# A decoder block on one core: the head's transfers in a fixed order, the mixing stage with `u` projected first, five gate tiles in one piece

## The chip, the core and the metric

The kernel runs on one core of a Trainium2 chip. The core's engines work side by side, each through an instruction list of its own: TensorE (PE, matrix products into PSUM), VectorE (DVE), ScalarE (ACT), GpSimd (POOL) and SyncE (SP, which here only issues transfers). Sixteen DMA engines move data between DRAM and SBUF. An instruction waits until the semaphores of what it needs have come; whatever stands behind it on the same engine waits with it.

The metric is the device time of one launch in microseconds (us), as the median of several runs. Besides, one execution is taken with the hardware profiler; all durations of single instructions come from that execution.

## The reference

One layer of a decoder over 512 tokens of width 1024, in fp32:

```
h = h + 1/2 * SwiGLU_1(RMSNorm(h))                 # ffn1, inner width 2816
z = RMSNorm(h) @ W_in                              # q | six k/v | branch gates | u
o = concat(NSA(q, k/v, gates), S5(u))              # 8 heads x 64  |  32 groups x 16 channels
h = h + o @ W_out
h = h + 1/2 * SwiGLU_2(RMSNorm(h))                 # ffn2
h = h + sigmoid(RMSNorm(h) @ W_gate) * (p @ W_ple)
out = RMSNorm(h)
```

NSA is an attention with three branches (compressed, selected and window keys), whose outputs are mixed by sigmoid gates. Its compressed keys come from a small network over windows of 32 tokens ("compression"). S5 is a complex linear recurrence over time with 64 states for each group of 16 channels, followed by a gelu and a gated product `y * sigmoid(y @ w_glu + b_glu)`.

## The kernel before

**Data.** `h` stays in SBUF for the whole run, transposed: 8 parts (`KT`) of 128 channels by 512 tokens. All weights lie in one DRAM array, `wpack`, in the order of use, cut into *units* of 128 x 1024 fp32 (512 KB). `load_unit` (L104) transfers one into a ring of four raw buffers; `unit` and `split` (L135 to L153) then make two matrices of it, `hi` (ScalarE, L151, the value rounded to the format that TensorE reads) and `lo = raw - hi` (VectorE, L152). The activations are split in the same way: `xh` on ScalarE, `xl` on VectorE (`split_k`, L171). Each product then is three products (`mm3`): hi by xh, hi by xl, lo by xh. One tile of 128 outputs by 512 tokens from 1024 inputs is 24 products of 512 columns, and closes a PSUM bank (tags A to D). Every product of the kernel is issued by the helper `mm`, so that all have line 130.

**Norms.** The split takes `h` times the gain; the scale of each token is put on later, after the product, where linearity allows it. `square` (L176) sums the squares of the parts on an adder (GpSimd in the head, VectorE elsewhere), `finish` (L190) sums over partitions by four small products on TensorE, takes the root (`rsqrt_steps`, L309) and spreads the result `rb` over all partitions by one more.

**Stages**, with their place in the profiled execution: the head (first transfers, splits and products, 0 to about 50 us), ffn1 (to 382; the constants of S5 are computed on VectorE beside it), the mixing stage (from the first `w_in` products, about 373, to about 621), the output projection and `p @ W_ple` (to about 655), ffn2 (to 998), the gate (998 to 1049) and the last norm and output (to 1063).

**The head.** Program order is unit 0, the eight parts of `h`, units 1 to 3 (L114 to L121). Unit 0 alone is split in two halves, so that products with its first half need not wait for all of it. The squares of parts 0 to 7 are added by seven steps on GpSimd (L184). VectorE also begins the chain of S5 constants here: small steps of 128 x 32 (L525 to L536, L552 and so on) on `prm`. The S5 tensor `s5o` in DRAM gets zeros by seven transfers that SP issues (L649).

**The mixing stage** (`mixer`, L794 to L1343) is written as Python generators, each step of which issues some instructions, and which `weave`, `chain` and `drain` interleave:
- `kq` (L969): two tiles of K with rotary embedding (six VectorE steps on 128 x 512 each, L959 to L964, a trip through DRAM, four `KA` copies and four `KB` subtractions, L976 and L977), then the first pair of Q tiles; `rotary(qd[1], "B")` is the second pair.
- `s5_input` (L852): four tiles of `u`; each is scaled (`ut`, L856), written to DRAM and read back as `u8` in another layout.
- `s5_in` and `s5_out` (L882, L910), for each of eight blocks of four groups: small products `ps_C<-u,fi`, eight VectorE steps on 256 columns (L894 to L897, L904 to L907), four scans (L900), then 16 small products and a copy; every second block `s5_back` (L923) transposes the output back.
- `cmp_kv` and `v_gates`: the remaining tiles of `w_in`. `cmp_all`: the compression. `glu` (L1079): first a gelu over S5's output and its split, then four tiles of the gated product, twelve products each.
- `scores` (L1121), for blocks 3 and 2 in one buffer pool and 1 and 0 later: products of Q with K in halves `QA,KA` (128 rows: 64 of hi and 64 of lo) and `QB,KB` (112 rows: 64 and 48 rows of an added term), a maximum on VectorE (L1155) and an exponential on ScalarE.
- `compressed`, `shifts`, `values`: the rest of the attention. `out_half`: the output projection, of which half the products (S5's half, `fill`) are put among the last steps of the attention.

In the kernel before the order is `kq`; the tiles of `u`; the second Q pair; then S5 woven with the scores of blocks 3 and 2, `cmp_kv` and `v_gates`; then the compression, with the gated product behind it.

**The gate** (L1396 to L1438): eight tiles of `sigmoid(norm(h) @ W_gate) * ple`, each in two halves of 256 tokens, all eight tiles for the first half and then all eight backwards for the second (which keeps eight split units in SBUF), so that the first half's last norm, scaling and output run beside the products of the second half.

**What sets the order.** `ENGINE_ORDER` lists, for each of the five engines, the positions of its instructions in the program as moves (step, and count of neighbours: `65:45` goes 65 ahead and takes 45 in a row), and `impose` (L1639) chains them:

```
            for _ in range(int(count or 1)):
                if before is not None:
                    tc.add_manual_dep(traced[at], before.name, follow, reason="order")
                before = traced[at]
                at += 1
```

So the generators above give the program's numbering and the buffers, while the list gives what an engine does first. `TILE_ORDER` adds pairs between engines. A transfer is an entry of SP's list like any other.

## Time and profile before

| | |
|---|---|
| median of 3 runs | 1063.21 us (1060.61 to 1064.24) |
| the profiled execution, its own time | 1064.68 us |
| its span | 1062.9 us |
| its granted TensorE clock | 0.986 |
| TensorE busy | 1026.4 us (97%), 6398 instructions |
| VectorE busy | 814.2 us (77%), 1369 instructions |
| ScalarE busy | 524.7 us (49%), 917 instructions |
| GpSimd busy | 81.9 us (8%), 100 instructions |
| DMA packets moved | 146.94 MB, mean 138 GB/s |

The span is the time from the first to the last recorded instruction; the execution's own time lies 1.8 us above it. The busy share is taken over the whole span and says little on one stage: the page therefore cuts the span into 40 slices of 26.6 us and gives a digit for each (9 is 90% or more), with the clock that TensorE was granted in tenths below. A window gives the same in us for any stretch. In the windows and groups "x" is a count; the mean of one instruction is given in ns; "idle before" is how long the engine did nothing ahead of it, with what ended the wait behind the arrow. The length of a TensorE instruction in the timeline is longer than its share of the pipeline: the distance between neighbouring starts is what counts.

### The profile page before, as it was taken

To read this page: it belongs to the slowest core of one execution; us is meant where nothing else is said; L and a number is where in the kernel's file an instruction comes from. 1 tells how busy PE (TensorE), PEld (TensorE's weight loads), DVE (VectorE), ACT (ScalarE), POOL (GpSimd) and SP (SyncE) were. 2 spreads that over 40 slices of the span, in tenths; PEclk is the share of its full clock that TensorE was granted. 3 is DMA by queue.
4 is the path that set the end of the run, shared out by engine and by line. 5 is a ranking of instruction groups with operands and counts; after the bars stand their busy time and mean duration, and the time that the engine had idled before them with its cause. 6 is when DMAs were issued, how large, how long until landed. Compare 5 with 4: busy or idle time off the path is not lost.

```text
span 1062.9 us, 16719 instructions
## 1 busy us (share of the span) xinstructions
PE 1026.4 (97%) x6398; PEld 899.3 (85%) x6398; DVE 814.2 (77%) x1369; ACT 524.7 (49%) x917; POOL 81.9 (8%) x100
## 2 busy tenths in 40 slices
PE   5999999999999999999899999999999999999995
PEld 4788899889989888886677787998899899899895
DVE  7799979777987675799798987875576467576776
ACT  5244256436425532257789856553355245245532
POOL 4000010001010100000000001001010001000000
PEclk9899999999999999999799999999999999999998
DMA  8332456757546836878210055447365545646202
GB/s 296 98 101 83 106 137 166 234 131 161 173 130 171 272 122 187 201 213 254 61 37 24 21 179 162 111 119 201 73 147 158 140 110 119 169 110 183 87 1 80
DMA packets 72128, 146.94 MB, mean 138 GB/s; under 512 B 19424, under 2 KB 30688, under 8 KB 71792
## 3 DMA queue, kind: packets, MB, share of 16 engines
q1 hardware_dynamic: 60512, 127.05, 38.4%
q0 software_dynamic: 10688, 18.65, 10.9%
q8 instruction: 50, 0.82, 0.3%
q10 hardware_dynamic: 848, 0.17, 0.1%
q14 instruction: 30, 0.25, 0.1%
HBM read 121.17 MB, written 15.73 MB: 129 GB/s over the span
## 4 chain that ended last, share of the span: by engine, by line
PE 86%; DVE 8%; issue 2%; ACT 2%; DMA 1%; POOL 0%; SPq 0%; POOLq 0%; DVEq 0%; ACTq 0%
PE ps_C L130 27%; PE ps_B L130 23%; PE ps_A L130 22%; PE ps_D L130 14%; DVE nmax L1155 1%; DVE lo L152 1%; DVE vv L900 1%; ACT xh L173 0%; DMA ti<-s5t 0%; DMA raw<-in_wpack 0%; DMA u<-ud 0%; PE ps_C L676 0%; ACT xn L183 0%; DMA h<-in_xT 0%; ACT hi L151 0%
## 5 line engine op out<-in xcount | busy, mean ns | idle before, releaser
L151 ACT CAST hi<-raw 128x1024 fp32r<-128x1024 f32 (+2 forms) x203 | 209.8, 1043 | 237.8 <-PE ps_C L130 92.7
L152 DVE TENSOR_TENSOR lo<-raw,hi 128x1024 fp32r<-128x1024 f32 (+2 forms) x203 | 243.3, 1210 | 44.4 <-ACT hi L151 43.4
L130 PE MATMUL ps_C<-hq,hi 128*128 128x512 f32 x704 | 218.6, 392 | 0.0
L130 PE MATMUL ps_A<-xh,hi 128*128 128x256 f32 (+1 forms) x456 | 142.6, 313 | 10.4 <-ACT hi L151 10.4
L130 PE MATMUL ps_A<-xh,lo 128*128 128x256 f32 (+1 forms) x456 | 142.5, 312 | 5.7 <-DVE lo L152 5.7
L130 PEld LDWEIGHTS ps_C<-hq,hi 128*128 128x128 f32 x704 | 127.1, 188 | 23.5 <-issue 0.8
L130 PE MATMUL ps_A<-xl,hi 128*128 128x256 f32 (+1 forms) x456 | 142.5, 312 | 0.0
L130 PE MATMUL ps_C<-hq,lo 128*128 128x512 f32 x352 | 137.2, 390 | 0.0
L130 PEld LDWEIGHTS ps_A<-xh,hi 128*128 128x128 f32 x456 | 87.2, 191 | 16.0 <-ACT hi L151 10.4
L130 PEld LDWEIGHTS ps_A<-xh,lo 128*128 128x128 f32 x456 | 87.4, 192 | 11.3 <-DVE lo L152 6.6
L130 PEld LDWEIGHTS ps_A<-xl,hi 128*128 128x128 f32 x456 | 87.2, 191 | 5.8 <-DVE xl L282 0.3
L130 PE MATMUL ps_B<-sh,hi 128*128 128x256 f32 x280 | 79.2, 283 | 0.0
L478 DVE SCALAR_TENSOR_TENSOR h<-ps_C,h 128x512 f32<-128x512 f32 x64 | 43.9, 688 | 45.9 <-PE ps_C L130 45.8
L130 PE MATMUL ps_B<-sl,hi 128*128 128x256 f32 x280 | 78.8, 281 | 0.0
L130 PE MATMUL ps_B<-sh,lo 128*128 128x256 f32 x280 | 78.4, 280 | 0.0
L130 PEld LDWEIGHTS ps_C<-hq,lo 128*128 128x128 f32 x352 | 66.1, 188 | 14.2
L354 POOL DMA_DIRECT2D raw<-in_wpack x35 | 31.6, 904 | 492.2 <-ACT sq L183 243.8
L130 PE MATMUL ps_D<-sh,hi 128*128 128x256 f32 x220 | 62.2, 283 | 0.0
L130 PE MATMUL ps_D<-sl,hi 128*128 128x256 f32 x220 | 61.9, 281 | 0.0
L130 PE MATMUL ps_D<-sh,lo 128*128 128x256 f32 x220 | 61.7, 280 | 0.0
L130 PE MATMUL ps_B<-xh,hi 128*128 128x512 f32 (+1 forms) x164 | 58.2, 356 | 0.0
L130 PE MATMUL ps_B<-xh,lo 128*128 128x512 f32 (+1 forms) x160 | 55.8, 349 | 0.0
(402 smaller groups left out, 2319.7 us busy)
## 6 DMA issues: line engine op xcount, KB each, us to landing
raw<-in_wpack SPq DMA_DIRECT2D x172, 512.0 KB, 4.2
raw<-in_wpack POOLq DMA_DIRECT2D x35, 256.0 KB, 4.7
raw<-raw POOLq DMA_DIRECT2D x35, 256.0 KB, 3.3
so<-s5o SPq DMA_DIRECT2D x8, 512.0 KB, 5.5
h<-in_xT SPq DMA_DIRECT2D x8, 256.0 KB, 4.9
s5f<-fs SPq DMA_DIRECT2D x4, 512.0 KB, 4.4
s5o<-gt SPq DMA_DIRECT2D x4, 512.0 KB, 3.5
s5t<-tcs SPq DMA_DIRECT2D x2, 1024.0 KB, 5.6
```

The source lines that it names most:

```text
L130: return PE.matmul(o, lhsT, rhs, start=start, stop=stop, **kw)
L151: S.copy(hi[:, c], raw[:, c])
L152: V.tensor_tensor(lo[:, c], raw[:, c], hi[:, c].bitcast(F32), OP.subtract)
L354: nc.gpsimd.dma_start(a0[:, 1], src[:, 0:512], accum_op=OP.add)
L478: V.scalar_tensor_tensor(h[:, m, :], o, 0.5, h[:, m, :], OP.mult, OP.add)
L900: V.tensor_tensor_scan(vv[:, g], r8[:, GC * j + g:GC * j + g + 1].to_broadcast([128, 64]), t1[:, g], 0.0, OP.mult, OP.add)
L1155: V.tensor_reduce(mc, s_, AX.X, OP.max, negate=True)
```

## The change

The program text changes in four places, and all lists of `ENGINE_ORDER` and `TILE_ORDER` are new.

**1. The head.** Ten small products of a matrix of ones with itself stand at the start of TensorE's list.

```diff
     for k in range(KT):
         nc.sync.dma_start(h[:, k, :], xv[:, k, :])
-        if k == 5:
-            load_unit(1, nc.sync)
+    load_unit(1, nc.sync)
     load_unit(2, nc.sync)
...
+    early = bank("D", (128, 128))
+    for _ in range(WARM):
+        mm(early, ones, ones, True, True)
...
+WARM = 10
```

In the lists: SP issued five parts of `h`, unit 0, a part, `prm`, unit 4 (which has a buffer outside the ring), two parts, unit 1, five zero writes, unit 2, small constants and zero writes, unit 3. After, it issues unit 0, part 0, unit 4, parts 1 to 7, units 1, 2 and 3, then `prm`, the other constants and units 5 to 8 of the list, and the seven zero writes behind these. ScalarE begins with one half of unit 0's `hi`, the square and `xh` of part 0 and the other half, and takes the squares of three parts among the first ten steps; part 7's `xh` is its fourteenth step. VectorE's splits of units 1 and 2 stand ahead of the chain of S5 constants (before: unit 2's behind its first half). GpSimd's seven additions stay as they are, behind squares that come earlier.

**2. The mixing stage.**

```diff
         def s5_input():
             for m in range(4):
                 o = proj("AD"[m % 2])
+                if m == 0:
+                    nm.finish()
+                    for t, raw in zip((cosr, sinr), ropes):
+                        V.tensor_tensor(t, raw, nm.rb, OP.mult)
...
-        drain(kq())
-        s5g, pg, cg, gg = s5_all(), chain(cmp_kv(), v_gates()), cmp_all(), glu()
-        sg = chain(scores(3, envs[3], mp, TS, G3), scores(2, envs[2], mp, "BC", G2))
+        s5g, pg, cg, gg = s5_all(), chain(kq(), rotary(qd[1], "B"), cmp_kv(), v_gates()), cmp_all(), glu()
+        s3, s2 = scores(3, envs[3], mp, TS, G3), scores(2, envs[2], mp, TS2, G2)
         drain(s5_input())
-        drain(rotary(qd[1], "B"))
         S.preload_act_table_set("exp_and_others")
-        weave((s5g, 17), (sg, S1), (pg, 6))
+        weave((s5g, 17), (pg, PROJ))
+        drain(pg)
         drain(s5g)
-        drain(pg)
-        drain(sg)
+        next(gg)
         s5x.close()
...
-        for _ in range(8):
-            next(cg)
+        next(s3)
+        next(s2)
+        sg = chain(s3, s2)
+        cg = chain(gg, cg)
+        weave((sg, S1), (cg, 12))
+        drain(sg)
```

The units of `wpack` stand in the new order of use. In TensorE's list: three products of `u` and the last 21 of ffn1's down projection; the rest of the 96 products of `u` with the five of the norm, and 42 of K and of the first Q pair; then S5's eight blocks beside the rest of K and Q, `cmp_kv` and `v_gates`. Behind S5's last block stand the first gated tile (12 products), nine products of the second, and only then the first scores, which alternate with the gated product and then the compression. More products of `fill` than before stand ahead of the attention's last blocks, and none is left between the last value products, where nine stood.

**3. Rows of the second K half.** `KB`, `KBc`, `QB` and `orow` are filled to 128 partitions (16 rows of zeros more), and all products with them read 128 rows instead of 112.

```diff
-                    mm(s_[:, i], QB[0:112, h0 + i], KBg[0:112, g, rs, :nk], False, False)
+                    mm(s_[:, i], QB[:, h0 + i], KBg[:, g, rs, :nk], False, False)
```

**4. The gate.** Five tiles are computed over all 512 tokens; the last three in two halves, as before.

```diff
+        whole = slice(0, SEQ)
+        for m in range(GATE_FULL):
+            if m:
+                gate_w.append(unit())
+            tile_of(m, whole, "AB"[m % 2], m == 0)
+            squared(m, whole, False)
+        for m in range(GATE_FULL, KT):
+            gate_w.append(unit(keep=gp))
         for hf in range(2):
             cs = slice(hf * HS, hf * HS + HS)
...
+            for m in range(GATE_FULL, KT):
+                tile_of(m, cs, "AB"[(m + hf) % 2], False)
+                sq = squared(m, cs, m == KT - 1)
             _, pb = rsqrt_rows([acc[:, cs], sq], 2)
...
+GATE_FULL = 5
```

`tile_of` and `squared` are the body of the old loop as functions of tile and columns. The gate thus issues 120 products of 512 columns and 144 of 256 where it issued 384 of 256 (120 fewer; ten come with the head). In the lists, the first gate tile's products are mixed with the last blocks of ffn2, and of the first half's eight final scaling steps five stand between the steps of the second half's last norm.

The lists of ffn1 and ffn2 are new as well, with the same instructions in them.

More of the change, by code (lines that the diff above doesn't have):

```diff
@@ L809, in mixer @@
         nc.scalar.dma_start(sel, a["sel"])
-        orow = mp.tile([48, 3], F32, name="orow")
+        orow = mp.tile([64, 3], F32, name="orow")
         nc.scalar.dma_start(orow, a["orow"])
@@ L820, in mixer @@
         for br in range(2):
-            V.tensor_copy(KB[64:112, 2 * br:2 * br + 2, :],
-                          orow[:, br + 1:br + 2, None].to_broadcast([48, 2, SEQ]))
+            V.tensor_copy(KB[64:128, 2 * br:2 * br + 2, :],
+                          orow[:, br + 1:br + 2, None].to_broadcast([64, 2, SEQ]))
         zero = mp.tile([128, 1], F32, name="zero")
@@ L951, in rotary @@
             oa = proj(tag)
-            if not hasattr(nm, "rb"):
-                nm.finish()
-                for t, raw in zip((cosr, sinr), ropes):
-                    V.tensor_tensor(t, raw, nm.rb, OP.mult)
             yield
@@ L1138, in scores @@
                                        OP.mult, OP.subtract)
-            S.copy(QB[64:112].rearrange("p h q -> p (h q)"), zero[64:112, 0:1].to_broadcast([48, 1024]))
+            S.copy(QB[64:128].rearrange("p h q -> p (h q)"), zero[64:128, 0:1].to_broadcast([64, 1024]))
             env.update(QA=QA, QB=QB)
@@ L1297, in mixer @@
         s1, s0 = scores(1, envs[1], ap_, "B"), scores(0, envs[0], ap_, "B")
-        for _ in range(8):
-            next(cg)
+        next(s3)
[4 more added lines that the diff above has]
+        drain(sg)
         next(s1)
         next(s0)
-        next(gg)
         drain(cg)
         c32 = compressed(3, 2)
-        for _ in range(2):
-            next(c32)
-            next(gg)
         cc = tp.tile([128, SEQ], FR, tag="rb1", name="cc")[:, :192].rearrange("p (q a c) -> p q a c", q=4, a=2)
@@ L1311, in mixer @@
         shifts(2, 4)
-        drain(gg)
         sg = chain(s1, compressed(1), s0, compressed(0))
@@ L1398, in block_kernel @@
         pad(gp, PADS[2])
-        gate_w = [unit(keep=gp)]
+        gate_w = [unit()]
         gf = gp.tile([128, KT], F32, tag="gf", name="gf", bufs=1)
@@ L1408, in block_kernel, with tile_of @@
         HS = SEQ // 2
+        def tile_of(m, cs, tag, first):
+            n = cs.stop - cs.start
+            wu = gate_w[m]
+            o = bank(tag)[:, :n]
+            for k in range(KT):
+                sl = slice(k * 128, (k + 1) * 128)
+                mm3(o, wu[0][:, sl], wu[1][:, sl], ng.xh[:, k, cs], ng.xl[:, k, cs], k == 0, k == KT - 1)
+            if first:
+                ng.finish()
+            t = gp.tile([128, SEQ], F32, tag="gt", name="gt")[:, :n]
+            V.tensor_tensor(t, o, ng.rb[:, cs], OP.mult)
+            S.activation(t, t, AF.Sigmoid)
+            V.tensor_tensor(t, t, ple[:, m, cs], OP.mult)
+            V.tensor_tensor(h[:, m, cs], h[:, m, cs], t, OP.add)
@@ new lines, in squared @@
+        def squared(m, cs, last):
+            n = cs.stop - cs.start
+            if m == 0:
+                S.activation(acc[:, cs], h[:, m, cs], AF.Square)
+                return None
+            sq = gp.tile([128, SEQ], F32, tag="gsq", name="gsq")[:, :n]
+            S.activation(sq, h[:, m, cs], AF.Square)
+            if not last:
+                V.tensor_tensor(acc[:, cs], acc[:, cs], sq, OP.add)
+            return sq
+        whole = slice(0, SEQ)
[4 more added lines that the diff above has]
+            squared(m, whole, False)
@@ L1409, in block_kernel @@
+        for m in range(GATE_FULL, KT):
+            gate_w.append(unit(keep=gp))
         for hf in range(2):
             cs = slice(hf * HS, hf * HS + HS)
-            for i in range(KT):
-                m = i if hf == 0 else KT - 1 - i
-                if hf == 0 and m:
-                    gate_w.append(unit(keep=gp if m < KT - 3 else None))
-                wu = gate_w[m]
-                o = bank("AB"[i % 2])[:, :HS]
-                for k in range(KT):
-                    sl = slice(k * 128, (k + 1) * 128)
-                    mm3(o, wu[0][:, sl], wu[1][:, sl], ng.xh[:, k, cs], ng.xl[:, k, cs], k == 0, k == KT - 1)
-                if i == 0 and hf == 0:
-                    ng.finish()
-                t = gp.tile([128, HS], F32, tag="gt", name="gt")
-                V.tensor_tensor(t, o, ng.rb[:, cs], OP.mult)
-                S.activation(t, t, AF.Sigmoid)
-                V.tensor_tensor(t, t, ple[:, m, cs], OP.mult)
-                V.tensor_tensor(h[:, m, cs], h[:, m, cs], t, OP.add)
-                if i == 0:
-                    S.activation(acc[:, cs], h[:, m, cs], AF.Square)
-                else:
-                    sq = gp.tile([128, HS], F32, tag="gsq", name="gsq")
-                    S.activation(sq, h[:, m, cs], AF.Square)
-                    if i < KT - 1:
-                        V.tensor_tensor(acc[:, cs], acc[:, cs], sq, OP.add)
@@ L1454 @@
 G2 = "r3", "ra"
-TW, TY, TP, TS = "C", "D", "D", "B"
-S1 = 34
+TW, TY, TP, TS, TS2 = "C", "D", "D", "B", "BC"
+PROJ = 12
+WARM = 10
+S1 = 32
 DEBUG_STOP = None
@@ L1695, in _pack_weights @@
     kk = np.concatenate([ks, kw], axis=1).reshape(D_MODEL, 4, 2, 32)
+    for m in range(4):
+        up_tile(u, m)
     for half in range(2):
@@ L1698, in _pack_weights @@
     for pair in range(2):
-        if pair:
-            for m in range(4):
-                up_tile(u, m)
         for half in range(2):
@@ L1709, in _pack_weights @@
     add(vt[:, 6:8])
+    m_major(x["s5_w_glu"][0], range(4), range(4))
     wk, wv = (x[n][0].reshape(16, 128, 256).transpose(1, 0, 2) for n in ("cmp_wk1", "cmp_wv1"))
@@ L1713, in _pack_weights @@
         add(np.concatenate([wk[:, 2 * i:2 * i + 2], wv[:, 2 * i:2 * i + 2]], axis=1))
-    m_major(x["s5_w_glu"][0], range(4), range(4))
     m_major(x["w_out"][0], range(8), range(4, 8))
@@ L1747, in prep @@
     sel = (rows[:, None] % 8 == np.arange(8)[None, :]).astype(f32)
-    orow = ((rows[:, None] // 8) % 3 == np.arange(3)[None, :]).astype(f32)
+    orow = np.concatenate([((rows[:, None] // 8) % 3 == np.arange(3)[None, :]).astype(f32), np.zeros((16, 3), f32)])
     def dup(v):
```

8 lines of the change are left out of this document (4 added, 4 removed), and 315 rows, old and new, of tables (ENGINE_ORDER, TILE_ORDER).

## The prediction

> **What bounds the kernel now.** I read the page first, then the windows of the stages that the change touches, then single rows. From the page: the busy tenths of TensorE (PE) and VectorE (DVE), the granted clock, and the chain of work that ended last.
>
> ```profile
> PE   5999999999999999999899999999999999999995
> DVE  7799979777987675799798987875576467576776
> PEclk9899999999999999999799999999999999999998
> PE 86%; DVE 8%; issue 2%; ACT 2%; DMA 1%; POOL 0%; SPq 0%; POOLq 0%; DVEq 0%; ACTq 0%
> ```
>
> The chain is 86% TensorE. The only slices below 9 are the first, the twentieth (505 to 531 us) and the last, and the clock falls to 7 or 8 tenths at the same places or next to them. So a change of order can win only what TensorE loses: the head, the mixing stage and the end. The windows give busy time and, in brackets, instructions for each engine, then the granted clock, the DMA share and GB/s.
>
> ```profile
> core 0: us, PE busy (x) PEld busy (x) DVE busy (x) ACT busy (x) POOL busy (x), PEclk, DMA share, GB/s
> 0.00:10.43 10.43, 0.00 (x0) 0.00 (x1) 3.92 (x10) 6.65 (x11) 1.70 (x9) 1.00 0.81 293
> 10.43:16.57 6.14, 6.14 (x15) 4.75 (x15) 5.90 (x19) 5.87 (x10) 0.19 (x1) 1.00 1.03 252
> 16.57:23.88 7.31, 7.31 (x34) 6.03 (x32) 7.10 (x10) 1.40 (x2) 6.92 (x6) 1.00 1.02 361
> 23.88:28.31 4.43, 0.39 (x2) 0.00 (x0) 4.36 (x9) 0.70 (x1) 2.45 (x2) 0.83 0.35 141
> 28.31:31.66 3.35, 3.35 (x8) 2.67 (x9) 3.04 (x15) 0.39 (x1) 0.00 (x0) 0.50 0.50 159
> 60.00:100.00 40.00, 40.00 (x179) 33.10 (x178) 37.50 (x98) 17.43 (x22) 0.00 (x0) 1.00 0.28 82
> 382.00:436.00 54.00, 54.00 (x241) 44.25 (x240) 34.56 (x53) 15.07 (x17) 1.75 (x2) 1.00 0.55 158
> 436.00:512.00 76.00, 69.93 (x511) 53.57 (x511) 73.54 (x170) 43.98 (x106) 0.00 (x0) 0.97 0.76 216
> 512.00:541.00 29.00, 26.60 (x151) 20.86 (x152) 22.30 (x55) 22.18 (x49) 0.00 (x0) 0.83 0.14 38
> 541.00:616.00 75.00, 75.00 (x367) 56.24 (x366) 68.38 (x133) 65.20 (x159) 0.00 (x0) 1.00 0.10 29
> 1000.00:1049.00 49.00, 48.28 (x402) 47.66 (x402) 37.50 (x89) 19.70 (x38) 1.73 (x2) 1.00 0.20 65
> ```
>
> Two things stand here. The head does no product for 10.43 us and then stalls again from 23.88 to 28.31. In the mixing stage VectorE has slack in one window and none in the next: 34.56 of 54 us before 436, then 73.54 of 76 us (0.968). Between 436 and 512 VectorE is the bound, with TensorE waiting for it. From 512 to 541 both wait on a chain of small steps (VectorE 0.77, clock 0.83).
>
> **The head.** Timeline rows: start, length, engine, line, what it writes and reads, and in brackets the idle time before it and its releaser.
>
> ```profile
> 7.71 5.93 SPq L649 DMA_DIRECT2D s5o<-zz  x5
> 13.68 0.63 SPq L111 DMA_DIRECT2D raw<-in_wpack  x1
> 3.77 1.28 ACT L173 ACT_TABLE_LOAD   x1 [3.77 <-DMA h<-in_xT]
> 5.06 1.97 ACT L173 ACTIVATE xh<-h,gains 128x512 fp32r<-128x512 f32 x3
> 10.43 0.79 PE L130 MATMUL ps_A<-xh,hi 128*128 128x512 f32 x1 [10.43 <-ACT hi L151]
> 27.04 1.22 DVE L152 TENSOR_TENSOR lo<-raw,hi 128x1024 fp32r<-128x1024 f32 x1
> 28.31 0.79 PE L130 MATMUL ps_A<-xh,lo 128*128 128x512 f32 x1 [4.04 <-DVE lo L152]
> 16.38 10.03 POOL L184 TENSOR_TENSOR acc<-acc,xn 128x512 f32<-128x512 f32 x7 [10.37 <-ACT xn L183]
> 18.26 1.34 DVE L536 SCALAR_TENSOR_TENSOR dt<-prm,ex 128x32 f32<-128x32 f32 x1
> 29.07 0.19 DVE L536 SCALAR_TENSOR_TENSOR r<-x,ex 128x32 f32<-128x32 f32 x1
> 100.60 23.80 PE ps_C L130 x105
> ```
>
> The last row, from the chain, prices a full product (512 columns): 23.80/105 = 0.227 us. TensorE loses before: 10.43 to the first product; 6.14 - 15 x 0.227 = 2.7 on 15 products at half clock; 4.43 - 2 x 0.227 = 4.0 in the stall; 3.35 - 8 x 0.227 = 1.5 at half clock behind it; less 0.4 in 16.57 to 23.88, where 34 products took 7.31 us. Sum 18.2.
>
> After: unit 0 is the first transfer. The first `h` part landed by 3.77 (it released the table load); a unit is twice its bytes, at 293 GB/s 0.9 us more, so 4.6. Table load to 5.9; ScalarE's list then has half of `hi`, a square, `xh` of part 0 and the other half. At 1.97/3 = 0.66 each that is 2.6: first product at 8.5. The part-7 `xh` is the 14th ScalarE step: 5.9 + 9.2 = 15.1, its `xl` 0.75 behind (estimate from the rows of the same size), so tile A closes at 15.9; its 24 products need 5.4, so 2.0 are lost on supply. Unit 1's `hi` follows at 16.1 and its `lo` at 17.3: 1.4 lost. The stall at 23.88 goes: units 2 and 3 were issued behind zero writes that held SP's queue for 5.93 us (the first row), now ahead of them, and unit 2's `lo` (27.04) now stands ahead of the S5 constants on VectorE. What is late next is the squares' sums on GpSimd, beside which a small VectorE step took 1.34 us (18.26) and alone 0.19 (29.07); the adds now start about 7 us earlier, on the splits. I charge one such wait, 1.2. Lost after: 8.5 + 2.0 + 1.4 + 1.2 = 13.1, **gain 5**. Bounds: 8 with no supply loss behind the first product, 1 if four adds lie on the path (4 x 1.15 more). The next use of what the moved zero writes write lies far behind the head; I cost them at nothing.
>
> The warm-up products cost nothing (TensorE is empty). Were the clock at half for the first 6 us, 15 products would be done at 14.6 and nine more by 16.7: they save 0.8, since supply sets the end of A.
> [...]
>
> **The mixing stage.** Down's last product; S5's first products (a tile's view: count, ns min/median/max, first and last start); its last ones (the chain); the gated product's first wait; then VectorE groups before 436 (three rows; count, busy, mean ns, idle before) and between 436 and 512 (three).
>
> ```profile
> 381.56 0.39 PE L130 MATMUL ps_C<-hq,lo 128*128 128x512 f32 x1
> L130 PE MATMUL ps_C<-u,fi x32: 217/275/276, 436.1 to 456.7; 128*128 128x64 f32 x32
> 511.98 1.91 PE ps_D L130 x16
> 509.10 0.79 PE L130 MATMUL ps_A<-ol,hi 128*128 128x512 f32 x1 [3.37 <-DVE ol L1085]
> L152 DVE TENSOR_TENSOR lo<-raw,hi 128x1024 fp32r<-128x1024 f32 x10 | 12.1, 1212 | 0.2 <-ACT hi L151 0.2
> L977 DVE TENSOR_TENSOR KB<-kf,KA 64x512 fp32r<-64x512 f32 x4 | 2.6, 678 | 0.2 <-ACT KA L976 0.2
> L963 DVE TENSOR_TENSOR r<-r,rb 128x512 f32<-128x512 f32 x2 | 1.4, 688 | 0.0
> L900 DVE TENSOR_TENSOR_SCAN vv<-r,t 128x64 f32<-128x64 f32 x32 | 7.4, 274 | 0.2
> L896 DVE TENSOR_TENSOR t<-ps_C,ti 64x256 f32<-64x256 f32 x8 | 3.4, 426 | 0.1
> L152 DVE TENSOR_TENSOR lo<-raw,hi 128x840 fp32r<-128x840 f32 (+2 forms) x5 | 5.2, 1048 | 0.1
> ```
>
> Down's last product starts at 381.56, with nine of the first projection's among it; after, three of `u`'s: down ends at 381.79 - 6 x 0.227 = 380.4. Then stand 93 products of `u`, 42 of K and Q and five of the norm ahead of S5's first: 135 x 0.227 + 1.4 = 32, so S5 starts at 412.4 instead of 436.1, into the window where VectorE idled 19.4 us. What moves behind that start is four splits (4.8), four `KB` copies (2.7) and eleven rotary steps at 0.688 (7.6; four more lay behind 436 already): 15.1 us. VectorE's work from there to 616 is then 73.54 + 22.30 + 68.38 + 15.1 = 179.3. Packed as 436 to 616 was before (164.2/180 = 0.912), the 110.9 ahead of the attention take 121.6 and the attention its 75: 412.4 + 196.6 = 609.0. Packed at 0.968, as between 436 and 512: 114.6 + 75, 602.0. Without idle, attention included: 591.7. What speaks for the better packing is that the gated product now lies beside the scores, so that the sparse stretch 512 to 541 gets company; against it, that TensorE has some 59 us of products beside S5 itself (sum of my own count of the list, at these prices), about as much as VectorE there. From 616 come off 7.0, 14.0 and 24.3. Output products that filled the end of the attention are pulled ahead, and nothing of the kind is left there: nine of them, 1.5 to 2 us, are charged. **Gain 8**, between the first two; bounds 0 (the rival below) and 22.
>
> The rows of the second K half go from 112 to 128 partitions: no instruction and no column more. No row differs in that alone; I take nothing, bounds 2 us either way (a tenth of 0.227 on some hundred products). The two ffn lists are rewritten without other work: nothing, bounds 3 us.
>
> **The gate.** First row from the timeline, second from the chain, third from the timeline.
>
> ```profile
> 1000.72 0.38 PE L130 MATMUL ps_A<-xh,lo 128*128 128x256 f32 x1 [1.68 <-DVE lo L152]
> 1016.88 1.42 PE ps_B L130 x12
> 1055.72 3.22 DVE L1436 SCALAR_TENSOR_TENSOR ple<-h,gf,ps_D 128x256 f32<-128x256 f32 x8 [1.32 <-PE ps_D L130]
> ```
>
> A half-width product takes 1.42/12 = 0.118. Five tiles in one piece make 120 full products of 240 halves: 28.3 - 27.2 = 1.1. The 1.68 us wait goes if unit 0's `lo` is ready, which now comes earlier, with gate products among the last of down. Against it: the first half's final scaling (eight at 0.40) now runs beside the last three tiles alone, and five of the eight lie within the last chain: 0.5 charged, at most 2.0. **Gain 2**, bounds -1 and 3.
>
> **Sum.** 5 + 8 + 2 = 15. The profiled execution took 1064.68 us for a span of 1062.9; it gives 1049.7. The median of the runs shown, 1063.21, is 1.5 lower: **1048**.
>
> **Rivals.** *A: the mixing packs fully.* With no idle on VectorE behind 412 the gain there is 14 to 22: 1033 to 1041. For it: 0.968 was reached for 76 us. Against: both engines would have to be full together.
>
> *B: the head's gain is given back.* The adds lie on the splits, four to seven at 1.15, and VectorE is 94% busy from 60 to 100, so what it owes there makes TensorE wait later. Head 0, mixing at its lower 5, gate 2: 1064.7 - 7 - 1.5 = 1056. For it: the 1.34 us row. Against: only three squares precede `xh` of part 7.
> [...]
>
> *C: slower, since the gated product's wall stands in TensorE's list.* All scores now come behind S5's last group and the first gated product; before they filled its waits. If a group keeps the pace it had with them, (511.98 - 436.1)/8 = 9.5 us, S5 ends at 488. VectorE still has 95.8 - 34.2 (scans 7.4, and eight lines of about 3.35, of which L896 is quoted) - 5.2 (splits) = 56.4 and the attention's 68.4, at 0.912 together 137: 625. The idle wait before the gated product (3.37 us before) halves the clock behind it, 29 x 0.17 = 5. So 14 us later than 616, less head and gate 7: 1064.7 + 7 - 1.5 = 1070. It decides from 8.7 us a group (8 x 8.7 + 412.4 + 137 + 5 = 616 + 8). Against: S5's own work, the moved steps and splits are (34.2 + 15.1 + 5.2)/8 = 6.8 us a group.
>
> *D: no difference.* S5 stays latency-bound at 9 us a group and the head gives 1: 1060 to 1066.
>
> **Chances.** Forecast (1041 to 1053) 0.47; A 0.17; B (1053 to 1060) 0.17; D 0.08; C 0.11. Faster by over 0.3% (3.2 us, about what a measurement of this kernel tells from no change) is forecast, A and B: 0.81; within it 0.08; slower 0.11. The range 1033 to 1062 leaves out C, about half of D and the lower edge of A: 0.2.
>
> **What would show it.** Right: first product near 8.5 and no wait over 2 us before 31; S5's first product near 412 and its last near 475; VectorE above 0.93 from 412 to 541; the gate's window 2.8 us shorter. Wrong: S5's last product later than 482, clock 0.5 behind the gated product's wait, small VectorE steps of 1.2 us among the splits before 17, or u's round trip through DRAM holding S5's first product.

## The result, and the profile after

The changed kernel takes 1050.58 us (median of 4 runs, 1050.21 to 1050.80), the kernel before 1063.72 in the same comparison: ratio 0.9882, 95% interval 0.9861 to 0.9902, so 13.1 us faster. The forecast was 1048, with 15 us to gain.

The page after the change: busy tenths of TensorE and VectorE, the granted clock, the chain that ended last.

```profile
PE   8999999999999999999999999999999999999995
DVE  7999888777988676999798888875576566576676
PEclk8999999999999999999999999999999999999997
PE 93%; DVE 3%; ACT 1%; issue 1%; DMA 1%; SPq 0%; POOLq 0%; POOL 0%; DVEq 0%; ACTq 0%
```

The hole at the twentieth slice and the low clock beside it are gone, the first slice went from 5 to 8, and VectorE's share of the chain fell from 8% to 3%. (TensorE's instructions went from 6398 to 6298: the profile counts each of the ten warm-up products twice, x20 in the head's timeline below.) The windows of the stages (columns as in those of before; `L129` is now the helper of all products):

```profile
0.00:8.00 8.00, 5.13 (x21) 4.53 (x21) 1.83 (x5) 4.22 (x7) 1.70 (x9) 1.00 0.79 273
8.00:16.00 8.00, 6.12 (x13) 3.64 (x14) 7.63 (x8) 8.00 (x14) 5.24 (x4) 0.57 1.04 400
16.00:24.00 8.00, 8.00 (x29) 6.38 (x28) 7.86 (x12) 2.41 (x4) 6.52 (x4) 0.79 0.70 228
408.00:470.00 62.00, 62.00 (x434) 52.15 (x434) 59.52 (x137) 20.24 (x38) 0.00 (x0) 1.00 0.70 205
470.00:500.00 30.00, 28.18 (x151) 19.67 (x151) 27.89 (x48) 27.80 (x60) 0.00 (x0) 1.00 0.38 102
500.00:535.00 35.00, 33.85 (x213) 23.58 (x210) 28.40 (x60) 27.77 (x71) 0.00 (x0) 1.00 0.68 208
535.00:604.00 69.00, 67.71 (x336) 50.24 (x335) 60.96 (x127) 60.21 (x150) 0.00 (x0) 1.00 0.06 16
988.00:1036.00 48.00, 46.67 (x281) 41.41 (x279) 35.02 (x70) 19.74 (x32) 1.74 (x2) 1.00 0.20 72
```

S5's blocks now lie in 408 to 470, where TensorE has no idle time at all and VectorE is busy for 0.96 of it. What is left stands in three places. In the head the clock is 0.57 from 8 to 16 us. From 470 to 535 TensorE is idle for 3.0 us. And 1.3 us of idle time stand in 535 to 604, where it had none before (541 to 616 there).

The head's timeline after (start, length, engine, line, operation, idle time before it and its releaser):

```profile
1.02 4.63 PE L129 MATMUL ps_D<-ones 128*128 128x128 f32 x20 [1.02 <-POOL ones L125]
7.00 0.49 PE L129 MATMUL ps_A<-xh,hi 128*128 128x512 f32 x1 [1.35 <-ACT hi L154]
8.39 0.50 PE L129 MATMUL ps_A<-xl,hi 128*128 128x512 f32 x1 [0.90 <-DVE xl L177]
10.09 0.80 PE L129 MATMUL ps_A<-xl,hi 128*128 128x512 f32 x1 [0.67 <-DVE xl L177]
14.19 0.79 PE L129 MATMUL ps_A<-xl,hi 128*128 128x512 f32 x1 [0.71 <-DVE xl L177]
19.68 0.40 PE L129 MATMUL ps_A<-xh,lo 128*128 128x512 f32 x1
8.71 8.45 DVE L177 SCALAR_TENSOR_TENSOR xl<-h,gains,xh 128x512 fp32r<-128x512 f32 x7 [0.37 <-ACT xh L176]
17.08 4.53 DVE L155 TENSOR_TENSOR lo<-raw,hi 128x1024 fp32r<-128x1024 f32 x2
9.95 2.97 POOL L187 TENSOR_TENSOR acc<-acc,xn 128x512 f32<-128x512 f32 x2 [0.47 <-ACT xn L186]
L177 DVE SCALAR_TENSOR_TENSOR xl<-h,gains,xh x8: 739/1036/1828, 7.6 to 15.4; 128x512 fp32r<-128x512 f32 x8
```

The first product comes at 7.00 instead of 10.43. But seven `xl` splits take 8.45 us, 1.21 each in the mean, and TensorE waits for them. The last line (a tile's view: count, ns min/median/max, first and last start; it has part 0's split as well) shows how uneven they are: in the trace the four that met an addition on GpSimd took 1.33 to 1.83 us, the others 0.74. The last product of tile A starts at 19.68.

From the stages, by the same instruction in both traces (ffn1's first output, before and after; down's last product after; the output projection's last product, before and after):

```profile
104.71 0.68 DVE L478 SCALAR_TENSOR_TENSOR h<-ps_C,h 128x512 f32<-128x512 f32 x1
99.20 0.69 DVE L481 SCALAR_TENSOR_TENSOR h<-ps_C,h 128x512 f32<-128x512 f32 x1 [0.22 <-PE ps_C L129]
374.12 0.39 PE L129 MATMUL ps_C<-hq,lo 128*128 128x512 f32 x1
642.02 0.39 PE L130 MATMUL ps_A<-oh,lo 128*128 128x512 f32 x1
630.71 0.39 PE L129 MATMUL ps_A<-oh,lo 128*128 128x512 f32 x1
```

The first output of ffn1 comes 5.5 us earlier. Down's last product (381.56 before) comes 6.1 us earlier when the products mixed into it are taken off (six fewer of them after, 0.227 each). The output projection ends 11.3 us earlier, the program 14.1. The expectations below give the second and third as 5.9 and 11.4.

### The profile page after: what moved, and what is told of

The parts are those of the page before. It is cut to its first block, busy times and chain, and to the rows that moved or that the text cites. A ratio compares the mean times of both kernels' runs of the same rounds, so it can differ in the third digit from the quotient of the medians.

```text
span 1048.8 us, 16515 instructions
## 1 busy us (share of the span) xinstructions
PE 1027.0 (98%) x6298; PEld 892.3 (85%) x6298; DVE 810.2 (77%) x1350; ACT 521.2 (50%) x907; POOL 82.5 (8%) x100
## 4 chain that ended last, share of the span: by engine, by line
PE 93%; DVE 3%; ACT 1%; issue 1%; DMA 1%; SPq 0%; POOLq 0%; POOL 0%; DVEq 0%; ACTq 0%
PE ps_C L129 28%; PE ps_A L129 26%; PE ps_B L129 25%; PE ps_D L129 14%; DMA h<-in_xT 1%; ACT xh L176 0%; DVE el L1253 0%; PE ps_C L679 0%; DVE ple L1450 0%; DVE xn L278 0%; DVE h L1422 0%; DVE gt L1421 0%; DVE nmax L1158 0%; DVE accf L1432 0%; ACT hi L154 0%
## 5 line engine op out<-in xcount | busy, mean ns | idle before, releaser
L129 PE MATMUL ps_C<-hq,hi 128*128 128x512 f32 x704 | 218.6, 391 | 0.0
L129 PEld LDWEIGHTS ps_C<-hq,hi 128*128 128x128 f32 x704 | 127.7, 188 | 24.2 <-DVE hq L348 0.6
L129 PE MATMUL ps_A<-xl,hi 128*128 128x256 f32 (+1 forms) x440 | 140.7, 320 | 2.4 <-DVE xl L177 2.3
L129 PE MATMUL ps_A<-xh,hi 128*128 128x256 f32 (+1 forms) x440 | 141.4, 321 | 1.4 <-ACT hi L154 1.4
L129 PE MATMUL ps_A<-xh,lo 128*128 128x256 f32 (+1 forms) x440 | 140.2, 319 | 0.0
L129 PE MATMUL ps_C<-hq,lo 128*128 128x512 f32 x352 | 137.3, 390 | 0.0
L129 PEld LDWEIGHTS ps_A<-xl,hi 128*128 128x128 f32 x440 | 84.0, 191 | 11.2 <-DVE xl L177 4.6
L129 PEld LDWEIGHTS ps_A<-xh,hi 128*128 128x128 f32 x440 | 83.9, 191 | 7.8 <-ACT hi L154 1.6
L129 PEld LDWEIGHTS ps_A<-xh,lo 128*128 128x128 f32 x440 | 84.1, 191 | 5.7 <-DVE lo L155 0.4
L129 PE MATMUL ps_B<-sh,hi 128*128 128x256 f32 x280 | 79.3, 283 | 0.0
L129 PE MATMUL ps_B<-sl,hi 128*128 128x256 f32 x280 | 78.8, 281 | 0.0
L129 PE MATMUL ps_B<-sh,lo 128*128 128x256 f32 x280 | 78.3, 280 | 0.0
L129 PEld LDWEIGHTS ps_C<-hq,lo 128*128 128x128 f32 x352 | 66.1, 188 | 14.3 <-DVE lo L155 0.2
L129 PE MATMUL ps_D<-sh,hi 128*128 128x256 f32 x220 | 62.0, 282 | 0.0
L129 PE MATMUL ps_D<-sl,hi 128*128 128x256 f32 x220 | 61.9, 281 | 0.0
L129 PE MATMUL ps_D<-sh,lo 128*128 128x256 f32 x220 | 61.6, 280 | 0.0
L363 POOL DMA_DIRECT2D raw<-raw x35 | 30.2, 862 | 341.2 <-DVE lo L155 310.5
L129 PEld LDWEIGHTS ps_B<-sh,hi 128*128 128x128 f32 x280 | 52.7, 188 | 0.9 <-issue 0.2
```

Of the source, the lines that this page charges most:

```text
L129: return PE.matmul(o, lhsT, rhs, start=start, stop=stop, **kw)
L363: nc.gpsimd.dma_start(a1[:, 1], a0[:, 1], accum_op=OP.add)
```

## The experiments

All runs are compared with the kernel before on the same chip; "to changed" is the difference of the medians. Intervals are 1.1 to 1.9 us to either side (2.2 for the changed kernel's own), and the kernel before itself came out between 1063.09 and 1064.01 in these comparisons. So a difference of 1.5 us or less from the changed kernel is not told from none by the times alone, and one of 2.4 us needs the trace beside it.

| run | median, us | ratio to before, 95% interval | to changed, us |
|---|---|---|---|
| undo_head | 1059.53 | 0.9970 (0.9956 to 0.9983) | +9.0 |
| undo_mixing | 1056.98 | 0.9945 (0.9933 to 0.9957) | +6.4 |
| undo_gate | 1053.01 | 0.9911 (0.9896 to 0.9925) | +2.4 |
| undo_ffn_lists | 1052.11 | 0.9899 (0.9885 to 0.9914) | +1.5 |
| head_alone | 1057.85 | 0.9948 (0.9935 to 0.9960) | |
| no_warmup | 1051.27 | 0.9888 (0.9874 to 0.9901) | +0.7 |
| adds_late | 1054.42 | 0.9918 (0.9904 to 0.9931) | +3.8 |
| adds_late_warm | 1055.72 | 0.9927 (0.9913 to 0.9940) | +5.1 |
| u_not_first | 1064.34 | 1.0013 (1.0003 to 1.0023) | +13.8 |
| fills_late | 1054.81 | 0.9918 (0.9904 to 0.9931) | +4.2 |
| head_v2 | 1052.96 | 0.9902 (0.9888 to 0.9915) | +2.4 |
| adds_on_vector | 1052.08 | 0.9901 (0.9883 to 0.9919) | +1.5 |

The engines' lists hold the same instructions, up to a cut, in both kernels at 72, 323, 650 and 997 us of before. So a stretch between two cuts can be given the order of either kernel. The diffs below show such a list in names, not in its coded moves.

### One part undone, and the head alone

**The head.**

```diff
-lists of SP, ACT, DVE, PE, POOL up to 72 us: changed; WARM = 10
+lists of SP, ACT, DVE, PE, POOL up to 72 us: before; WARM = 0
```

> The changed kernel with the head undone: until 72 us every engine's list is that of before (transfers, splits, squares), and the ten warm-up products are left out. My theory: the head's gain is kept to the end, and the end of ffn1's down projection, which stands 5.9 us earlier in the changed kernel when the products mixed into it are taken off, moves back by that much: 1056.5 us (1055.5 to 1057.5), ratio to before 0.994. Rival 1, the head's gain is given back before the mixing stage: 1050.5 to 1052. Rival 2, an earlier head also lets transfers and VectorE run ahead so that the mixing gains from it: 1058 or more.

Measured 1059.53: 9.0 us, 3 more than the lead at the end of ffn1. The reason shows at the first output of ffn1, in the run and in the one with the head alone:

```profile
106.99 0.69 DVE L481 SCALAR_TENSOR_TENSOR h<-ps_C,h 128x512 f32<-128x512 f32 x1 [0.21 <-PE ps_C L129]
```

```profile
98.75 0.68 DVE L481 SCALAR_TENSOR_TENSOR h<-ps_C,h 128x512 f32<-128x512 f32 x1
```

The head of before in front of the new ffn1 list gives it at 106.99, later than the kernel before itself (104.71): the new list expects what the new head leaves behind. The new head in front of the list of before gives it at 98.75. The time is that of the expectation's rival 2 (1058 or more), but not for its reason: in the two profiled executions down's last product comes 7.8 us later than in the changed kernel (381.89 against 374.12), the output projection's and the span's end both 7.9, so the mixing adds nothing.

```diff
 kernel before, all lists behind 72 us
+lists of SP, ACT, DVE, PE, POOL up to 72 us: changed; WARM = 10
```

> The kernel before with the head alone changed: until 72 us every engine's list is the changed one, with the ten warm-up products; ffn lists, mixing (112 rows) and gate as before. Undoing the head in the changed kernel cost 9.0 us, more than the 5.9 by which ffn1's down projection ended earlier. My theory: the head by itself is worth about 6, and the other 3 are the mismatch of the head of before with the new ffn1 list (its first ffn1 output came at 107.0, against 104.7 in the kernel before): 1057 us (1056 to 1058.5), ratio 0.9945. Rival 1, the head is worth 9 wherever it stands: 1054. Rival 2, its lead is lost again in ffn1's list of before: 1060 to 1063.

Measured 1057.85, against 1063.09 of the kernel before in that comparison: 5.2 us. So the head is worth 5 to 6, and the rest of the 9 is mismatch (2.3 us of it stand at ffn1's first output, 106.99 against 104.71). Undoing a part of a hand-written order measures the part and its fit; putting it alone into the old kernel measures it without that.

**The mixing stage.**

```diff
-drain(s5_input()); weave((s5g, 17), (pg, PROJ)); next(gg); weave((sg, S1), (cg, 12)); 128 rows
+drain(kq()); drain(s5_input()); drain(rotary(qd[1], "B")); weave((s5g, 17), (sg, S1), (pg, 6)); 112 rows
```

> The changed kernel with the mixing stage undone: its program, the order of its units and all lists from 323 to 650 us are those of before, with 112 rows for the second K half; head, ffn lists and gate stay as changed. My theory: the output projection ended 11.4 us earlier in the changed kernel, 5.9 of them from the head, so the mixing is worth 5.5 (not the 8 of the forecast): 1056 us (1055 to 1057.5). Rival 1, the forecast's 8: 1058.5. Rival 2, the mixing gives nothing by itself, the rest comes from what stands earlier and later: 1050.5 to 1052.

Measured 1056.98: 6.4 us, within the expected range and under the forecast's 8. The rows above give 11.3 - 6.1 = 5.2 up to the output projection. This undoes all of the stage at once; what the 128 rows, the gated product ahead of the scores and the earlier `fill` are worth one by one was not run.

**The gate.**

```diff
-for m in range(GATE_FULL): tile_of(m, whole, ...); then three tiles in halves
+for hf in range(2): for i in range(KT): a tile of 256 columns
```

> The changed kernel with the gate undone: its loop and the lists behind ffn2 (from 997 us of before) are those of before. My theory: fewer and longer products (1.1) and the wait for the first lo (1.7), less what the tail loses: 1052.3 us (1051.5 to 1053.3). Rival, the tail takes all back: 1050.6 within 0.5. If the count of products were worth nothing and only the wait went: 1051.5.

Measured 1053.01: 2.4 us. The wait of before is back, to the hundredth:

```profile
989.23 0.38 PE L129 MATMUL ps_A<-xh,lo 128*128 128x256 f32 x1 [1.68 <-DVE lo L155]
```

From the gate's last product to the end of the span it is 13.9 us in this run and 14.7 in the changed kernel, so the tail takes 0.8 back: 1.7 + 1.1 - 0.8 = 2.0 of the 2.4. The other 0.4 isn't the gate's: the same product early in ffn2 already comes 0.5 us later in this run (667.88 against 667.34), ahead of the lists that were undone.

**The lists of ffn1 and ffn2.**

```diff
-lists from 72 to 323 us and from 650 to 997 us: changed
+lists from 72 to 323 us and from 650 to 997 us: before
```

> The changed kernel with the lists of ffn1 (72 to 323 us) and of ffn2 (650 to 997 us) of before; head, mixing and gate as changed. My theory: the two are worth nothing, 1050.6 within 1.0; the trace shows the lead 0.9 larger at the end of ffn2 than at its beginning, so at most 1051.5. Rival, the rewritten lists are needed to keep the head's gain, since VectorE is 94% busy there: 1053 to 1056.

Measured 1052.11, 1.5 us, between the expectation and its rival and at the edge of what the times can tell; the trace agrees with it (down's last product at 375.45, against 374.12 in the changed kernel).

### What bounds the mixing stage

```diff
-u0 u1 u2 u3 | kA kB qA | S5 blocks beside kB qA qB kc vc v0..v3
+kA kB qA | u0 u1 u2 u3 | qB | S5 blocks beside kc vc v0..v3
```

> The changed kernel with the order of before for the projections alone: K and the first Q pair, then u, then the second Q pair stand ahead of S5's first block (23 us of products and 17.8 us of VectorE steps come ahead of it again); the gated product still stands ahead of the scores and of the compression. My theory (VectorE and TensorE both bound the S5 blocks, so work taken from them shortens them): S5 starts 23 us later and its blocks take about 43 us instead of 63, net 3 us slower: 1053.6 us (1051.5 to 1056). Rival 1, the whole gain of the mixing (6) comes from projecting u first: 1057. Rival 2, S5's blocks are a chain of small steps that cannot go faster than 7.9 us each: 1070 or more. Rival 3, projecting u first is worth nothing: 1050.6.

Measured 1064.34, 13.8 us slower than the changed kernel and no faster than the kernel before. S5's first product comes at 430.3 instead of 407.4 and its last 13.2 us later. So the blocks became 9.7 us shorter, not the 20 that I had expected, and none of the four expected times was met. The windows ahead of S5 and over it, and waits of TensorE in it:

```profile
431.00:482.00 51.00, 42.98 (x325) 36.14 (x325) 46.44 (x117) 15.11 (x30) 0.00 (x0) 0.87 0.65 204
408.00:431.00 23.00, 23.00 (x107) 19.14 (x106) 11.03 (x13) 4.40 (x5) 0.00 (x0) 1.00 0.52 147
```

```profile
434.46 1.07 PE L129 MATMUL ps_C<-u,fi 128*128 128x64 f32 x8 [2.28 <-DVE t L899]
439.35 0.70 PE L129 MATMUL ps_D<-so,z 128*64 128x128 f32 x4 [3.35 <-DVE z L910]
```

VectorE is the bound of S5's blocks here (46.44 of 51 us), with TensorE idle for 8.0 us of them, 7.3 in waits that VectorE ended, and at a clock of 0.87. Ahead of them VectorE idles for 12 of 23 us, and for 21.8 us in all from 376 to 431; in the changed kernel it idles for 12.7 us from 376 to S5's start. There the same 23 us of K and Q products lie inside the blocks, where TensorE would wait.

This also says what the two parts of the stage are worth together. With both undone the kernel is at 1056.98. With `u` not first, but the scores taken out of S5's blocks, it is 7.4 us slower than that. In the kernel before, the scores filled TensorE's waits in S5. Taken out alone, they leave the waits empty; with the K and Q products put in their place, the stage gains 6. (The lists of this run were made for the changed order, so a part of the 7.4 can be mismatch, as with the head; that was not separated.)

The second doubt was the end of the attention, where the products of `fill` are used up. Waits there in the changed kernel, 1.98 us of idle time (the expectation reckons 2.65 from the distances of the starts):

```profile
603.72 0.50 PE L129 MATMUL ps_C<-QA,KA 128*128 128x512 f32 x1 [0.69 <-ACT e L1247]
606.16 0.47 PE L129 MATMUL ps_D<-eh,VLc 128*128 128x512 f32 x1 [0.55 <-ACT eh L1251]
608.61 0.50 PE L129 MATMUL ps_D<-el,VL 128*128 128x512 f32 x1 [0.74 <-DVE el L1253]
```

```diff
 PE list:  ... fill x9 (570 to 576 us) ... QA,KA | eh,VLc | el,VL
+PE list:  ... QA,KA behind fill x3 | eh,VLc behind fill x3 | el,VL behind fill x3
```

> The changed kernel with the last nine products of the first output half moved from 570 to 576 us behind the attention's last value products, three each ahead of the three products that waited 1.04, 0.71 and 0.90 us there; one split on ScalarE and one addition on VectorE go behind them with it. My theory (the used-up fills cost what they cost): 2 us of products go into 2.65 us of waits: 1048.8 us (1048.3 to 1049.8). Rival 1, their old place then shows the same wait: 1050.6 within 0.5. Rival 2, the split that now comes later holds the output projection: 1051 or more.

Measured 1054.81, 4.2 us slower. Rival 1 came true in part, and rival 2 in its time, though what held the output projection was the addition and not the split.

```profile
571.22 0.50 PE L129 MATMUL ps_C<-QA,KA 128*128 128x512 f32 x1 [0.35 <-ACT eh L1251]
574.78 0.50 PE L129 MATMUL ps_C<-QA,KA 128*128 128x512 f32 x1 [0.41 <-ACT eh L1251]
576.72 0.50 PE L129 MATMUL ps_C<-QA,KA 128*128 128x512 f32 x1 [0.51 <-ACT eh L1251]
612.44 0.79 PE L129 MATMUL ps_A<-oh,hi 128*128 128x512 f32 x1 [2.41 <-DVE h L1116]
```

Where the nine products stood there are three new waits of 1.27 us together. The addition that I put behind the attention's last steps on VectorE frees a PSUM bank, and the output projection waits 2.41 us for it, more than the three waits that were filled. Behind that wait the products run at half clock (a mean of 0.79 from 612 to 620 us, some 1.7 us more). How much the move alone is worth, with the addition left in place, wasn't tried.

### What bounds the head

**The warm-up products.**

```diff
-WARM = 10
+WARM = 0
```

> The changed kernel without the ten warm-up products. In its profile the clock is full for the first four products (7.0 to 9.4) and half from 10.1 to 19.4, since the waits for the xl splits let it fall again. My theory: the warm-up saves nothing to speak of, 1050.6 within 0.8. [...]

Measured 1051.27, 0.7 us more, not told from none.

```profile
6.92 0.80 PE L129 MATMUL ps_A<-xh,hi 128*128 128x512 f32 x1 [6.92 <-ACT hi L154]
```

The first product takes 0.80 us in this run and 0.49 in the changed kernel, and neighbours start 0.43 us apart instead of 0.23. With the warm-up the first four products run at full clock; behind the waits of 0.90 and 0.67 us for `xl` they start 0.43 us apart there too (10.68 and 11.11 us). (A window's clock is 1.00 where the trace has no record of the clock yet, as in this run up to 20.7 us and in the kernel before up to 16.6; there the distance of the starts shows half.)

**The squares behind the splits.** GpSimd's additions follow ScalarE's squares (`sq`), so their place is set in ScalarE's list.

```diff
-ACT: hi0 acc<-h0^2 xh0 hi0 sq1 xh1 xh2 sq2 sq3 xh4 xh3 xh6 xh5 xh7 hi1 sq4 hi2 sq5 sq6 sq7 hi3
+ACT: hi0 xh0 hi0 xh1 xh2 xh4 xh3 xh6 xh5 xh7 hi1 acc<-h0^2 hi2 sq1 sq2 sq3 sq4 sq5 sq6 sq7 hi3
```

> The changed kernel with ScalarE's order in the head changed: the squares of parts 0 to 3 stand behind the xh of part 7 and unit 1's hi, so that GpSimd's adds begin behind the xl splits. In the changed kernel seven xl splits took 8.45 us (1.21 each) beside the adds, the same splits 0.75 each alone. My theory (adds hold the splits): the seven take 5.3 to 6, the last ends near 14 instead of 17.1, and tile A, at half clock from about 7 (24 products at 0.427), closes near 17.3 instead of 19.9: 1048 us (1047 to 1049). Rival 1, the clock alone paces tile A: less than 0.8 gained, 1050. Rival 2, the sum of squares comes too late and the norm waits: 1050.6 or more.

Measured 1054.42: the mechanism was right and the result was the other way. Rows of VectorE (the seven `xl` in a tile's view, the last three in the timeline, then steps of the S5 constants) and, in the second fence, of TensorE (tile A's last product and its next two waits) in this run's timeline:

```profile
L177 DVE SCALAR_TENSOR_TENSOR xl<-h,gains,xh x7: 744/751/752, 8.1 to 13.5; 128x512 fp32r<-128x512 f32 x7
12.13 2.08 DVE L177 SCALAR_TENSOR_TENSOR xl<-h,gains,xh 128x512 fp32r<-128x512 f32 x3 [0.56 <-ACT xh L176]
...
17.73 0.18 DVE L529 TENSOR_SCALAR ex<-ex 128x32 f32<-128x32 f32 x1
17.94 1.16 DVE L530 TENSOR_SCALAR ex<-ex 128x32 f32<-128x32 f32 x1
...
23.00 1.27 DVE L535 SCALAR_TENSOR_TENSOR ex<-ex,ex 128x32 f32<-128x32 f32 x1
24.19 0.17 DVE L537 CAST exi<-ex 128x32 int32<-128x32 f32 x1
24.30 2.98 DVE L535 SCALAR_TENSOR_TENSOR ex<-ex,ex 128x32 f32<-128x32 f32 x5
```

```profile
14.73 0.39 PE L129 MATMUL ps_A<-xh,lo 128*128 128x512 f32 x1
23.13 0.50 PE L129 MATMUL ps_B<-xh,lo 128*128 128x512 f32 x1 [2.51 <-DVE lo L155]
27.07 1.86 PE L129 MATMUL ps_D<-ones,acc 128*128 128x1 f32 x8 [2.74 <-POOL acc L187]
```

The splits take 0.75 each without the additions beside them (0.69 from one to the next), and tile A's last product starts at 14.73 instead of 19.68. But the additions now lie beside the small steps of the S5 constants, and many of these take 1.2 us there instead of 0.2: the five steps of one `scalar_tensor_tensor` line that start at 24.30 take 2.98 us, 0.60 each in the mean, between steps of 0.17 and of 1.27. The price in VectorE's time is the same as before, one meeting for each addition: counted step by step in the two traces, the seven additions cost it 7.0 us in the changed kernel (four `xl` 3.7, two `lo` 2.2, one small step 1.1) and 7.2 us here (seven small steps). What changed is who waits. The additions end at 27.0 instead of 22.8 us. Unit 3's `lo`, which stands among the small steps, is late by 2.51 us, the norm's products wait 2.74 us for the sum (rival 2), and behind them the clock is low (0.54 from 24 to 32 us).

**The same with the clock held.**

```diff
 the list with the late squares
-PE: ones x10, A x24
+PE: ones x14, (A x3, ones x2) five times, A x9
```

> As the run with the late squares, with fourteen warm-up products at the start (until about 7.5) and two more behind each of the first five groups of three products, so that TensorE is hardly ever idle between 1 and 13 us. My theory: the clock stays full, tile A closes with the splits, near 14.5: another 2 to 3 us, 1045.5 (1044.5 to 1047). Rival 1, the transfers of the h parts pace the splits (DMA share above 1.0 from 8 to 16 us): tile A not before 16, 1047 to 1048. Rival 2, the clock falls all the same: as the run with the late squares.

Measured 1055.72.

```profile
8.00:16.00 8.00, 7.86 (x42) 6.46 (x43) 6.28 (x9) 7.34 (x11) 0.00 (x0) 1.00 1.05 403
```

The clock is full from 8 to 16 us, but tile A's last product now starts at 16.03 rather than 14.73, as the additional products take their own time (0.36 us from the start of each of the five pairs to the next product); the two waits behind it stay (1.93 and 2.44 us).

**The late squares with the order behind them mended.**

```diff
 the list with the late squares
-PE: A0 x24, B0 x12, A1 x6, B0 x3, B1 x3, A1 x3, norm x4, A1 x9, B0 x9, ...
+PE: A0 x24, B0 x24, A1 x24, B1 x6, norm x4, B1 x18, C2 x12, norm x1, ...
-DVE: lo1 lo2, 7 constants, lo3, 49 other steps, lo4, ...
+DVE: lo1 lo2, 3 constants, lo3, 11 constants, lo4, ...
```

> The changed kernel with the late squares, and what that run showed to be late next taken care of: on TensorE the second tile, the third and six products of the fourth stand ahead of the norm's four small products, and twelve products of the fifth ahead of its last; unit 3's lo and unit 4's lo stand further ahead among VectorE's constants, and unit 3's hi ahead of four squares. My theory: tile A closes near 15 (19.9 as changed) and no wait over 0.7 us follows until 33; some 5 us earlier, 1045.5 us (1044.5 to 1047.5). Rival 1, the norm is late all the same (sum of squares not before 27): TensorE waits near 32 and the run gives 1049 to 1051. Rival 2, VectorE owes its constants and TensorE pays between 45 and 100: 1048 to 1050.

Measured 1052.96. TensorE doesn't wait between 10 and 40 us, and then:

```profile
40.32 0.79 PE L129 MATMUL ps_C<-xh,lo 128*128 128x512 f32 x1 [2.84 <-DVE lo L155]
```

The time is later than both rivals' (1048 to 1051), and the mechanism is a piece of each: the `lo` stands on VectorE behind the norm's result (39.06, the result at 37.06), and VectorE is busy for 12.11 of the 13 us from 32 to 45.

**No additions on GpSimd.**

```diff
-                    n1.square(k, G, rows[k])
+                    n1.square(k, V, rows[k])
```

> The changed kernel with the seven additions of the squares on VectorE (0.68 us each) instead of GpSimd, put behind the xl splits and the lo of units 1 and 2; squares late on ScalarE; the norm's four small products behind the second tile and six products of the third on TensorE, its last one behind six of the fourth; the norm's steps, and the lo of units 3 to 5, further ahead among VectorE's constants. In the changed kernel VectorE's steps beside the adds took about 7 us more than alone (seven xl 3.2, two lo 2.1, two small steps 2.0); the additions cost it 4.8. My theory: with no adds beside it VectorE is 2 us ahead where it was the bound of the run with the second order (TensorE waited 2.84 us at 40.3 for a lo behind it), and TensorE can use its earlier tile A: 1046.5 us (1045 to 1048.5). Rival 1, VectorE is still too late in places where TensorE's list now runs ahead of it: 1049 to 1052, no better than as changed. Rival 2, the lead is lost between 45 and 100 us, where VectorE is over 94% busy: 1049 to 1051, with TensorE's waits there.

Measured 1052.08, no better than the changed kernel (rival 1). Two TensorE rows of this run:

```profile
23.03 1.05 PE L129 MATMUL ps_D<-ones,acc 128*128 128x1 f32 x8 [0.86 <-DVE acc L187]
49.34 0.79 PE L129 MATMUL ps_A<-xh,lo 128*128 128x512 f32 x1 [3.35 <-DVE lo L155]
```

TensorE starts the last product of the sixth tile 3.8 us earlier than in the changed kernel (45.15 against 48.92). It loses that lead in one wait of 3.35 us for a `lo`, and in the half clock behind it (a mean of 0.89 from 45 to 60 us). In the windows VectorE is busy for 14.54 of those 15 us:

```profile
45.00:60.00 15.00, 11.65 (x46) 9.20 (x45) 14.54 (x20) 5.79 (x8) 0.00 (x0) 0.89 0.23 71
```

So TensorE's start is not what bounds the head: in these orders VectorE's list up to 60 us is, and three orders that put TensorE 4 to 5 us ahead at the end of tile A all gave it back. In head_v2 and in this run the late `lo` stands behind ffn1's own steps on VectorE, a row of them 0.7 us each. Whether it can stand ahead of more of them, or more of VectorE's work can move behind 60 us, wasn't tried. No run was faster than the changed kernel.

## Why the prediction was right, and where it was off

**The sum.** 15 was forecast, 13.1 measured: head 5 (5.2 alone), mixing 8 (6.4 undone, 5.2 by the trace), gate 2 (2.4, of which 2.0 by the trace), ffn lists 0 (1.5, within the 3 allowed). The measured parts don't add up to the whole (15.5 with the head alone, 19.3 with the head undone), since each run also measures the fit of what is left. The forecast's mechanisms stand in all three; its rivals A, C and D did not come about. B did in part, inside the head's own 5.

**The head: right sum, with luck.** The first product came at 7.00, not 8.5: the table load no longer waited for a transfer (it began at 1.17 us), and I had put it behind unit 0. Tile A ended at 19.9, not at 15.9. I had charged one wait of 1.2 beside the additions; in VectorE's time the seven splits lost 7 x (1.21 - 0.75) = 3.2 and the two `lo` behind them 4.53 - 2 x 1.22 = 2.1. And the clock was at half from 10.1 to 19.4 in spite of the warm-up. The additions thus cost VectorE more than the price I took; the splits at 0.75 without additions beside them (adds_late) agree with that. Behind tile A the waits that I had charged (1.4 and 1.2) did not come. Counted as in the prediction, TensorE lost 19.9 - 5.4 = 14.5 up to the end of tile A, not 13.1 in all. But the sum for before was short as well: it ends at 31.66, and the clock was at half until 33.6 (about 1.0 us) and a wait of 0.28 followed at 41.37. So 18.2 and 13.1 were both about 1.4 too small, and that their difference came out at 5 is luck.

The warm-up was worth 0.7, where the forecast said 0.8. With it, products ran at half clock (0.63 us for 0.39) from 10.1 us on, behind waits of 1.35, 0.90 and 0.67 us with a product or a few between them. By the trace's own records the clock was full from 5.75 to 9.16 us and half to 19.40; in the first of these stretches TensorE was idle for about 2.1 us in two waits. How much idle time it takes for the clock to fall, the runs do not settle.

**The mixing: the place right, the size off.** S5 started at 407.4, which is the forecast's 412.4 less the head's 5 (by the rows the lead was 6.1 at the end of ffn1, so about 1 was lost on the way). Its last product came at 469, as forecast ("near 475") less the same 5; VectorE was busy for 0.96 of the blocks. So a block took 7.7 us, under the 8.7 from which rival C decides. The step that was mis-sized is what follows. The stretch 470 to 535, which I priced at 0.912 to 0.968 of VectorE's time, ran at 56.29/65 = 0.87 (27.89 and 28.40 in the two windows), and 535 to 604 at 60.96/69 = 0.88. So the sign named for being right, VectorE above 0.93 from 412 to 541, was not met (117.98 of 129 us, 0.915). The used-up products at the end of the attention cost 2.0 us of idle time in three waits, as charged (1.5 to 2). The 112 rows made no difference, as forecast: the mean of the 34 products `QB,KB` of 512 columns is 395 ns before and 393 ns after.

What the forecast had not seen is that the two halves of this part need each other: it priced the K and Q products only as work that moves, and u_not_first shows that they are what fills TensorE's waits once the scores are gone.

**The gate.** The wait of 1.68 us and the count of products were right (the gate's last product comes 3.2 us earlier than in undo_gate; less the 0.5 from ahead of ffn2 and the wait, 1.0 is left for the count, where 1.1 was reckoned); the tail took 0.8 back where 0.5 was charged.

## What to carry to other kernels

When one filler is taken out of a chain of small steps, look first for what will fill TensorE's waits instead; here the two edits were worth 6 us together and cost 7 with one of them missing. Where two engines were both busy at more than nine tenths, as in this head (from 8 to 50 us TensorE 0.96, VectorE 0.97), a lead of one of them was not worth anything: find whose queue holds the next operand, and price that queue. And undo a part of a hand-made order in both directions (out of the new kernel, into the old one), since the order behind it was made for what stood before it.

## What the runs showed of the hardware that was not expected

An addition on GpSimd cost the VectorE step that it met about the same whether the step was long or short, some 1.0 us in these two runs (the changed kernel and adds_late): of the splits of 128 x 512 (0.74 alone) three of the four that met one took 1.77 to 1.83 us and the fourth 1.33, two `lo` took 2.30 instead of 1.22, and steps of 128 x 32 took 1.14 to 1.29 instead of about 0.18. So the seven additions cost VectorE 7.0 us beside the splits and 7.2 beside the short steps; putting them off moved the price to other steps and did not lower it, and the kernel was slower because of who then waited. And TensorE's clock fell to half behind waits of which the longest was 1.35 us, and was back at full at 19.4, when the products had run without a pause from 14.2 us on; in the run with the late squares, where no further wait came, half clock lasted from 7.9 to about 10.9 us.
